# A conformer's last 256 channels, convolved as two halves of 128 tokens

## The chip, the cores and the metric

The kernel runs on one core of one Trainium2 chip. The metric is the device time of one execution in microseconds (us), and the figure quoted is the median over runs. In the rows below PE is TensorE's matrix multiplication, PEld its weight loads, DVE is VectorE, ACT is ScalarE, POOL is GpSimd, and SP is SyncE, which issues most DMA.

## The reference, cut to what matters

The program computes two blocks of a network over one sequence of 256 tokens with 1024 features, in float32. The first block has four layers; layer 1 mixes tokens with this conformer convolution (one of it in the program), and an MLP follows:

```python
def causal_depthwise_conv(x, w):
    k = w.shape[0]                       # 31 taps, one weight per tap and channel
    return lax.conv_general_dilated(x, w[:, None, :], window_strides=(1,),
        padding=[(k - 1, 0)], dimension_numbers=("NWC", "WIO", "NWC"),
        feature_group_count=x.shape[-1])

def conformer_conv_mixer(x, w_pw1, b_pw1, w_dw, b_dw, ln_g, ln_b, w_pw2, b_pw2):
    h = x @ w_pw1 + b_pw1
    a, gate = jnp.split(h, 2, axis=-1)
    h = a * jax.nn.sigmoid(gate)
    h = causal_depthwise_conv(h, w_dw) + b_dw
    mean = jnp.mean(h, axis=-1, keepdims=True)
    var = jnp.mean(jnp.square(h - mean), axis=-1, keepdims=True)
    h = (h - mean) * lax.rsqrt(var + LN_EPS) * ln_g + ln_b
    h = jax.nn.silu(h)
    return h @ w_pw2 + b_pw2
```

The LayerNorm is taken over all 1024 channels of a token, so it needs every channel's convolution, but only of that token.

## The kernel before

The 256 tokens are two halves, h = 0 and h = 1, of 128 tokens, one token per partition. Each half runs through a generator of its own. A driver hands both the same stream of weight units (128 x 1024 values, cast by ACT and DVE into a high part `wh`/`whx` and a low part `whl`/`whxl`); the second half lags five units behind the first in these layers. The multiplication is `mm3` (its matmuls are all on L59): three fp32r matmuls per 128 x 512 piece, `wh` and `whl` with the high part `t2h` of the activations, and `wh` with their low part `t2l`.

In the conformer (`conformer`), the first product gives 256 channels at a time, c = 0 to 3, with their gates, in a tile `cfr` per half. When both halves of a c are there, `depthwise` is put on a list of side work that is stepped between the products. For 256 channels and all 256 tokens it

- transposes the gates and the values (`tp<-ident,cfr`), takes the sigmoid on ACT (`cfs`) and multiplies on DVE into `win`, channels on partitions, 30 zeros ahead of the tokens;
- splits the 31 taps: for the first `CF_PE[c]` taps ACT (odd k) or POOL (even k) writes a diagonal matrix `dg` of that tap's weights, six buffers in turn, and PE multiplies it with the shifted window into PSUM (`mm<-win,dg`, plain float32); the other taps are multiply-adds on DVE into `cvo` (L711, started by L699), two blocks b of 128 channels each;
- adds the two sums (L715). For c = 3 the split is 15 taps on PE, 16 on DVE.

When the convolution of c = 3 is done, the half's generator goes on: the 1024 channels are transposed back (`tp<-ident,cvo`, L66), DVE takes the statistics (`bn`, L640), POOL the power (`rstd`, L411), DVE normalizes (`cfz`, L747), PE transposes again (`tp<-ident,cfz`), ACT applies SiLU (`cff`, L754) and casts (`t2h`, L351), DVE makes `t2l` (L352). This happens for two groups of 512 channels, and then the second product, eight weight units `cf2`, runs into `acc`. Half 1 does the same five units later.

Each engine executes its instructions in one fixed order; a scheduler settles that order when the program is built, from the order of the code and the buffers.

Of the kernel before, what the change touches and what calls it, by code (L numbers as in the profile page):

```python
# [10 lines left out]
F32 = mybir.dt.float32  # L11
# [4 lines left out]
ALU = mybir.AluOpType  # L16
# [3 lines left out]

PACE = {"1": (5, 2, 8), "A": (5, 2, 8), "M": (0, 4, 6), "B": (3, 2, 6), "P": (6, 1, 8)}

CF_PE = (10, 11, 13, 15)
RAWP, WHP = 3, 4
EXTRA = {"1": (2, 4), "A": (2, 4), "M": (0, 2)}

# [24 lines left out]
class Builder:  # L51
# [616 lines left out]
        s.segs.append((len(s.plan), None, None))  # L668
        s.plan_linear(s.io["cf_w_pw2"][j], 8, "cf2")

    def depthwise(s, c, raws):

        nc, sh = s.nc, s.sh
        on_pe = CF_PE[c]
        yield
        tg = s.tpb((128, 2, 2, 128))
        for h in range(2):
            for b in range(2):
                nc.tensor.transpose(tg[:, h, b, :], raws[h][:, 256 + 128 * b:384 + 128 * b], s.ident)
        sg = s.B2((128, 2, 2, 128), "cfs")  # L680
        for b in range(2):
            q = 2 * c + b
            nc.scalar.activation(sg[:, :, b, :], tg[:, :, b, :], AF.Sigmoid, bias=s.cfb1[:, 8 + q:9 + q])
        ta = s.tpb((128, 2, 2, 128))
        for h in range(2):
            for b in range(2):
                nc.tensor.transpose(ta[:, h, b, :], raws[h][:, 128 * b:128 * b + 128], s.ident)
        win = s.pool.tile([128, 2, 286], F32, tag="win", bufs=2, name="win")
        nc.gpsimd.memset(win[:, :, 0:30], 0.0)
        for b in range(2):  # L690
            q = 2 * c + b
            nc.vector.scalar_tensor_tensor(win[:, b, 30:286].rearrange("p (h t) -> p h t", h=2), ta[:, :, b, :],
                                           s.cfb1[:, q:q + 1], sg[:, :, b, :], op0=ALU.add, op1=ALU.mult)
        o = s.B2((128, 2, 256), "cvo")
        ps = s.mmb((128, 2, 256))
        for b in range(2):
            w = s.cfw[:, 2 * c + b, :]
            yield
            nc.vector.tensor_scalar(o[:, b, :], win[:, b, on_pe:on_pe + 256], w[:, on_pe:on_pe + 1],  # L699
                                    s.cfbd[:, 2 * c + b:2 * c + b + 1], op0=ALU.mult, op1=ALU.add)  # L700
            rest = list(range(on_pe + 1, 31))
            for k in range(on_pe):
                dg = s.pool.tile([128, 128], F32, tag="dg", bufs=6, name="dg")
                if k % 2:
                    nc.scalar.mul(dg, s.ident, w[:, k:k + 1])
                else:
                    nc.gpsimd.tensor_scalar(dg, s.ident, w[:, k:k + 1], None, op0=ALU.mult)
                nc.tensor.matmul(ps[:, b, :], dg, win[:, b, k:k + 256], start=k == 0, stop=k == on_pe - 1)
                n = len(rest) * (k + 1) // on_pe - len(rest) * k // on_pe
                for m in rest[len(rest) * k // on_pe:][:n]:  # L710
                    nc.vector.scalar_tensor_tensor(o[:, b, :], win[:, b, m:m + 256], w[:, m:m + 1], o[:, b, :],  # L711
                                                   op0=ALU.mult, op1=ALU.add)
                if k % 2:
                    yield
        nc.vector.tensor_tensor(o, o, ps, op=ALU.add)  # L715
        sh["cf", c] = o

    def conformer(s, h, lhs, rin, j):
        nc, sh = s.nc, s.sh
        for c in range(4):  # L720
            p = s.acc()
            for k in range(0, 8, 2):
                W = yield "cf1"
                for kk in range(2):
                    s.mm3(lhs, k + kk, W, [(p, kk * 512, 512, k + kk == 0, k + kk == 7)])
            t = s.B2(name="cfr")
            nc.scalar.mul(t, p, rin)
            sh["cfr", c, h] = t
            if h:
                s.side.append([s.depthwise(c, [sh.pop(("cfr", c, e)) for e in range(2)]), ("cf", c - 1) if c else None, 0.0])  # L730
        cb = s.layer_vec(("cb2", j), s.io["cf_b_pw2"][j])
        yield "#"
        while ("cf", 3) not in sh:
            s.side_step(False)
        t = slice(128 * h, 128 * h + 128)
        tps = []
        for g in range(2):
            p = s.tpb()
            for b in range(4):
                nc.tensor.transpose(p[:, b, :], sh["cf", 2 * g + b // 2][:, b % 2, t], s.ident)  # L740
            tps.append(p)
        flat = [p.rearrange("p b c -> p (b c)") for p in tps]
        r, m = s.ln_stats(flat, 1e-5)
        hT = []
        for c in range(2):
            z = s.B2(name="cfz")
            zi = nc.vector.tensor_scalar(z, flat[c], m, r, op0=ALU.subtract, op1=ALU.mult)  # L747
            if c == 0 and h == 0:
                s.hold = s.split_to, zi.ins
            tz = s.tr(z)  # L750
            f = s.B2((128, 4, 128), "cff")
            for b in range(4):
                q = 4 * c + b
                nc.scalar.activation(f[:, b, :], tz[:, b, :], AF.Silu, scale=s.cfg[:, q:q + 1], bias=s.cfbb[:, q:q + 1])  # L754
            hT.append(s.split(f))
        ps = yield from s.linear(hT, 8, "cf2")
        out = []
        for g in range(2):
            t = s.B2(name="cfo")
            nc.vector.tensor_tensor(t, ps[g], cb[g], op=ALU.add)  # L760
            out.append(t)
        return out
# [1148 lines left out]
```

## Time and profile before

| what | value |
|---|---|
| median of 3 runs | 2991.22 us (2991.18 to 2991.85) |
| the profiled execution's own time | 2988.3 us |
| its span, first to last instruction | 2986.5 us |
| PE busy | 2906.1 us, 97% of the span |
| DVE busy | 1982.2 us, 66% |
| ACT busy | 1522.5 us, 51% |
| POOL busy | 211.8 us, 7% |
| mean granted TensorE clock | 0.995 of full |

Busy time is an average over stages that differ: the change touches one stretch, from about 486 to 545 us after the span's start, and what counts there is which engine the others wait for. A granted clock of 1.00 is 2.4 GHz, 0.50 is 1.2 GHz. Matmuls of plain float32 stand in the trace as two records each.

### The profile page before, as it was taken

To read this page: it belongs to the slowest core of one execution; us is meant where nothing else is said; L and a number is where in the kernel's file an instruction comes from. 1 tells how busy PE (TensorE), PEld (TensorE's weight loads), DVE (VectorE), ACT (ScalarE), POOL (GpSimd) and SP (SyncE) were. 2 spreads that over 40 slices of the span, in tenths; PEclk is the share of its full clock that TensorE was granted. 3 is DMA by queue.
4 is the path that set the end of the run, shared out by engine and by line. 5 is a ranking of instruction groups with operands and counts; after the bars stand their busy time and mean duration, and the time that the engine had idled before them with its cause. 6 is when DMAs were issued, how large, how long until landed. Compare 5 with 4: busy or idle time off the path is not lost. (4 is left out here: it accounts for less than half of the span.)

```text
span 2986.5 us, 49201 instructions
## 1 busy us (share of the span) xinstructions
PE 2906.1 (97%) x18698; PEld 2335.4 (78%) x18698; DVE 1982.2 (66%) x3159; ACT 1522.5 (51%) x2348; POOL 211.8 (7%) x352
## 2 busy tenths in 40 slices
PE   8999998999999999999999999999999999999998
PEld 6778877787788878888877777878778787777886
DVE  7666678666766766766557757665665676667656
ACT  4354554555544534544447664444444387544443
POOL 0000024000000000200001000000010000000000
PEclk9999999999999999999999999999999999999999
DMA  7457852687578655886766233477667552334773
GB/s 240 155 175 236 240 164 78 191 238 213 177 233 241 188 169 169 239 250 198 224 196 184 75 114 108 127 220 224 212 207 224 160 173 87 100 113 140 238 225 125
DMA packets 342733, 542.64 MB, mean 182 GB/s; under 512 B 71381, under 2 KB 205729, under 8 KB 342496
## 3 DMA queue, kind: packets, MB, share of 16 engines
q1 hardware_dynamic: 333824, 514.90, 57.4%
q0 software_dynamic: 8096, 22.49, 2.6%
q8 instruction: 147, 2.41, 0.3%
q10 hardware_dynamic: 576, 2.10, 0.2%
q14 instruction: 90, 0.74, 0.1%
HBM read 516.30 MB, written 23.07 MB: 181 GB/s over the span
## 5 line engine op out<-in xcount | busy, mean ns | idle before, releaser
L59 PE MATMUL acc<-wh,t2h 128*128 128x512 f32 (+1 forms) x1512 | 610.8, 404 | 9.9 <-ACT t2h L351 7.3
L59 PE MATMUL acc<-whl,t2h 128*128 128x512 f32 (+1 forms) x1512 | 593.7, 393 | 0.4 <-DVE whl L224 0.4
L224 DVE TENSOR_TENSOR whl<-raw,wh 128x1024 fp32r<-128x1024 f32 x341 | 414.5, 1217 | 244.9 <-ACT wh L223 221.7
L223 ACT CAST wh<-raw 128x1024 fp32r<-128x1024 f32 x341 | 356.9, 1047 | 392.6 <-PE acc L59 246.5
L59 PE MATMUL acc<-wh,t2l 128*128 128x512 f32 (+1 forms) x1512 | 512.3, 395 | 3.1 <-DVE t2l L352 2.2
L224 DVE TENSOR_TENSOR whxl<-raw,whx 128x1024 fp32r<-128x1024 f32 x272 | 329.7, 1214 | 217.4 <-ACT whx L223 190.7
L223 ACT CAST whx<-raw 128x1024 fp32r<-128x1024 f32 x272 | 284.3, 1046 | 291.7 <-PE acc L59 135.4
L59 PEld LDWEIGHTS acc<-wh,t2h 128*128 128x128 f32 x1512 | 285.7, 189 | 82.5 <-ACT t2h L351 17.9
L59 PE MATMUL acc<-whx,t2h 128*128 128x512 f32 (+1 forms) x856 | 343.9, 403 | 2.1 <-ACT t2h L351 1.4
L59 PEld LDWEIGHTS acc<-wh,t2l 128*128 128x128 f32 x1512 | 283.6, 189 | 69.8 <-DVE t2l L352 9.2
L59 PE MATMUL acc<-whxl,t2h 128*128 128x512 f32 (+1 forms) x856 | 335.4, 392 | 0.1
L59 PEld LDWEIGHTS acc<-whl,t2h 128*128 128x128 f32 x1512 | 285.7, 189 | 55.7 <-issue 1.0
L59 PE MATMUL mm<-whx,t2h 128*128 128x512 f32 x800 | 313.4, 392 | 3.1 <-ACT whx L223 2.5
L59 PE MATMUL mm<-whxl,t2h 128*128 128x512 f32 x800 | 311.7, 390 | 0.8 <-DVE whxl L224 0.8
L59 PE MATMUL mm<-whx,t2l 128*128 128x512 f32 x800 | 311.6, 389 | 0.6 <-DVE t2l L352 0.6
L59 PE MATMUL acc<-whx,t2l 128*128 128x512 f32 (+1 forms) x856 | 282.4, 391 | 1.1 <-DVE var L644 0.7
L224 DVE TENSOR_TENSOR whxl<-rawx,whx 128x1024 fp32r<-128x1024 f32 x142 | 173.0, 1219 | 127.5 <-ACT whx L223 116.8
L224 DVE TENSOR_TENSOR whl<-rawx,wh 128x1024 fp32r<-128x1024 f32 x145 | 177.2, 1222 | 110.4 <-ACT wh L223 97.5
L223 ACT CAST whx<-rawx 128x1024 fp32r<-128x1024 f32 x142 | 148.8, 1050 | 158.9 <-PE mm L59 92.3
L223 ACT CAST wh<-rawx 128x1024 fp32r<-128x1024 f32 x145 | 152.2, 1051 | 151.2 <-PE acc L59 101.5
L59 PEld LDWEIGHTS acc<-whx,t2h 128*128 128x128 f32 x856 | 161.3, 188 | 39.7 <-ACT t2h L351 5.5
L59 PEld LDWEIGHTS acc<-whx,t2l 128*128 128x128 f32 x856 | 160.4, 188 | 38.0 <-DVE t2l L352 2.6
(617 smaller groups left out, 4103.3 us busy)
## 6 DMA issues: line engine op xcount, KB each, us to landing
raw<-in_mlp_w SPq DMA_DIRECT2D x153, 512.0 KB, 4.6
raw<-in_w_in SPq DMA_DIRECT2D x128, 512.0 KB, 3.7
raw<-in_ffn_w SPq DMA_DIRECT2D x216, 256.0 KB, 3.7
rawx<-in_mlp_w SPq DMA_DIRECT2D x103, 512.0 KB, 4.6
rawx<-in_ffn_w SPq DMA_DIRECT2D x136, 256.0 KB, 3.9
raw<-in_ret_w_in SPq DMA_DIRECT2D x58, 512.0 KB, 4.5
raw<-in_ffn_w SPq DMA_DIRECT2D x53, 512.0 KB, 4.2
rawx<-in_ret_w_in SPq DMA_DIRECT2D x38, 512.0 KB, 4.4
```

The costliest lines, as they stand in the source:

```text
L59: r = m0(out, a, b, **k)
L223: c = nc.scalar.copy(wh[:, 0:n], r[:, 0:n])
L224: nc.vector.tensor_tensor(wl[:, 0:n], r[:, 0:n], wh[:, 0:n].bitcast(F32), op=ALU.subtract)
```

## The change

For c = 3, `depthwise` is called once per half of the tokens instead of once for both. The first call makes `win` and the output tile `o`, computes tokens 0 to 127 and leaves both tiles for the second call, which computes tokens 128 to 255. Half 0's generator waits for ("cf", 3, 0) alone, and half 1's for ("cf", 3, 1). The second call may start once the first is done. The number of taps on PE for c = 3 goes from 15 to 17, and in the calls for one half ACT writes three of four `dg` tiles instead of one of two.

```diff
-CF_PE = (10, 11, 13, 15)
+CF_PE = (10, 11, 13, 17)
...
-    def depthwise(s, c, raws):
+    def depthwise(s, c, raws, halves=(0, 1)):
...
+        nh = len(halves)
         yield
-        tg = s.tpb((128, 2, 2, 128))
-        for h in range(2):
+        tg = s.tpb((128, nh, 2, 128))
+        for h in range(nh):
...
-        win = s.pool.tile([128, 2, 286], F32, tag="win", bufs=2, name="win")
-        nc.gpsimd.memset(win[:, :, 0:30], 0.0)
+        if halves[0] == 0:
+            win = s.pool.tile([128, 2, 286], F32, tag="win", bufs=2, name="win")
+            nc.gpsimd.memset(win[:, :, 0:30], 0.0)
+            o = s.B2((128, 2, 256), "cvo")
+            sh["cfw", c] = win, o
+        else:
+            win, o = sh.pop(("cfw", c))
+        t0, n = 128 * halves[0], 128 * nh
...
-        ps = s.mmb((128, 2, 256))
+        ps = s.mmb((128, 2, n))
         for b in range(2):
             w = s.cfw[:, 2 * c + b, :]
+            at = lambda k: win[:, b, k + t0:k + t0 + n]
+            ob = o[:, b, t0:t0 + n]
...
-                if k % 2:
+                if k % 2 or nh == 1 and k % 4:
                     nc.scalar.mul(dg, s.ident, w[:, k:k + 1])
                 else:
                     nc.gpsimd.tensor_scalar(dg, s.ident, w[:, k:k + 1], None, op0=ALU.mult)
-                nc.tensor.matmul(ps[:, b, :], dg, win[:, b, k:k + 256], start=k == 0, stop=k == on_pe - 1)
+                nc.tensor.matmul(ps[:, b, :], dg, at(k), start=k == 0, stop=k == on_pe - 1)
...
-        nc.vector.tensor_tensor(o, o, ps, op=ALU.add)
-        sh["cf", c] = o
+        nc.vector.tensor_tensor(o[:, :, t0:t0 + n], o[:, :, t0:t0 + n], ps, op=ALU.add)
+        for h in halves:
+            sh["cf", c, h] = o
...
-            if h:
-                s.side.append([s.depthwise(c, [sh.pop(("cfr", c, e)) for e in range(2)]), ("cf", c - 1) if c else None, 0.0])
+            if c == 3:
+                s.side.append([s.depthwise(c, [sh.pop(("cfr", c, h))], (h,)), ("cf", *((3, 0) if h else (2, 1))), 0.0])
+            elif h:
+                s.side.append([s.depthwise(c, [sh.pop(("cfr", c, e)) for e in range(2)]), ("cf", c - 1, 1) if c else None, 0.0])
...
-        while ("cf", 3) not in sh:
+        while ("cf", 3, h) not in sh:
             s.side_step(False)
```

What stands in the engines' queues moves in one place of the program. On PE, at the convolution of c = 3 (`dg`) and its neighbours, the difference reads:

```order
 L59 MATMUL mm<-win,dg 128x256 x22
-L66 MATMUL tp<-ident,cfr 128x128 x8
+L66 MATMUL tp<-ident,cfr 128x128 x4
 L66 MATMUL tp<-ident,cvo 128x128 x4
-L59 MATMUL mm<-win,dg 128x256 x30
+L59 MATMUL mm<-win,dg 128x128 x34
 L66 MATMUL tp<-ident,cvo 128x128 x4
 L66 MATMUL tp<-ident,cfz 128x128 x4
```

So 30 matmuls over 256 tokens became 34 over 128 ahead of half 0's LayerNorm, and the other half's transposes are gone from there.

Further down PE's queue, in half 0's second product (`acc<-wh`, units 3 to 5 of it), the changed kernel has:

```order
L59 MATMUL mm<-win,dg 128x128 x6
L59 MATMUL acc<-wh,t2l 128x512 x2
L59 MATMUL mm<-win,dg 128x128 x2
...
L59 MATMUL acc<-whx,t2l 128x512 x2
L59 MATMUL mm<-win,dg 128x128 x4
...
L59 MATMUL acc<-whx,t2l 128x512 x2
L59 MATMUL mm<-win,dg 128x128 x22
L66 MATMUL tp<-ident,cvo 128x128 x8
```

All 34 matmuls of the second half's convolution stand here, behind half 0's whole LayerNorm chain and its first three units, and ahead of half 1's `cvo` transposes. Four more `cfr` transposes stand just before, among units 1 and 2. In the kernel before, nothing but the products of units 0 to 5 stood ahead of `tp<-ident,cvo 128x128 x8`.

On ACT, from the first half's diagonals to half 1's SiLU, the changed kernel has:

```order
L714 ACTIVATE dg<-ident,cfc 128x128 x24
L765 ACT_TABLE_LOAD
L765 ACTIVATE cff<-tp,cfc 128x128 x4
L351 CAST t2h<-cff 128x512
L223 CAST whx<-raw 128x1024
L765 ACTIVATE cff<-tp,cfc 128x128 x4
L351 CAST t2h<-cff 128x512
L685 ACT_TABLE_LOAD
L685 ACTIVATE cfs<-tp,cfc 128x128 x2
L714 ACTIVATE dg<-ident,cfc 128x128 x20
L765 ACT_TABLE_LOAD
L765 ACTIVATE cff<-tp,cfc 128x128 x4
```

Before, the last `cff` x4 followed the second `t2h` directly; the sigmoid of the second half with two table loads and 20 diagonals now stand between. DVE's queue has the same form: `win` x2, L708 x2, L720 x26 and the sum of the second half stand behind half 0's second `t2l` and ahead of half 1's `bn`. Behind half 1's LayerNorm the rows of all engines are those of before.

## Rows read from the trace of the kernel before

**Rows 1.** Stretches: us; busy PE, PEld, DVE, ACT, POOL (count); clock, DMA share, GB/s.

```profile
487.00:500.00 13.00, 13.00 (x60) 11.38 (x61) 13.00 (x33) 5.70 (x12) 10.96 (x13) 1.00 0.01 2
500.00:508.00 8.00, 1.94 (x9) 1.06 (x7) 6.71 (x11) 1.59 (x5) 0.57 (x1) 0.76 0.08 13
508.00:515.00 7.00, 6.05 (x17) 4.50 (x18) 5.87 (x7) 3.71 (x7) 0.00 (x0) 0.54 0.93 320
515.00:520.00 5.00, 5.00 (x24) 4.12 (x23) 0.06 (x1) 0.00 (x0) 0.00 (x0) 1.00 0.46 160
...
527.00:533.00 6.00, 5.74 (x20) 4.67 (x21) 2.64 (x3) 3.39 (x7) 0.00 (x0) 0.72 0.04 5
```

**Rows 2.** What PE waited for from 470 to 570: total us, times, longest.

```profile
PE acc L59 <- ACT t2h L351: 4.3, 2, 2.2
PE tp L66 <- DVE cfz L747: 3.6, 3, 2.8
```

**Rows 3.** Timeline of DVE: start, duration, instruction, idle before and its releaser.

```profile
486.39 0.47 DVE L692 SCALAR_TENSOR_TENSOR win<-tp,cfc,cfs 128x256 f32<-128x256 f32 x1
...
487.77 0.72 DVE L699 TENSOR_SCALAR cvo<-win,cfc 128x256 f32<-128x256 f32 x2
488.42 12.34 DVE L711 SCALAR_TENSOR_TENSOR cvo<-win,cfc,cvo 128x256 f32<-128x256 f32 x30
500.68 0.69 DVE L640 BATCH_NORM_STATS2 bn<-tp 128x6 f32<-128x512 f32 x1
501.28 0.66 DVE L715 TENSOR_TENSOR cvo<-cvo,mm 128x512 f32<-128x512 f32 x1
```

**Rows 4.** Timeline of PE over the same stretch.

```profile
487.00 13.19 PE L59 MATMUL mm<-win,dg 128*128 128x256 f32 x60 [0.69 <-DVE win L692]
...
508.59 0.79 PE L59 MATMUL acc<-wh,t2h 128*128 128x512 f32 x1 [2.25 <-ACT t2h L351]
```

**Rows 5.** DVE groups by form: count, busy us, mean ns, idle before.

```profile
L1478 DVE SCALAR_TENSOR_TENSOR gcv<-win,rwpar,gcv 128x128 f32<-128x128 f32 x144 | 38.9, 344 | 2.2 <-ACT gcv L1476 2.1
L901 DVE TENSOR_TENSOR glu<-silu,mm 128x256 f32<-128x256 f32 x88 | 35.8, 407 | 4.6 <-ACT silu L899 4.6
...
L802 DVE SCALAR_TENSOR_TENSOR scu<-swin,cfc,scu 128x128 f32<-128x128 f32 x32 | 9.1, 343 | 0.0
...
L800 DVE TENSOR_SCALAR scu<-swin,cfc 128x128 f32<-128x128 f32 x16 | 3.8, 280 | 0.5 <-ACT swin L796 0.4
```

**Rows 6.** Timeline of PE at 102 us, float32 matmuls of 128 columns.

```profile
101.94 1.95 PE L59 MATMUL mm<-rT 128*128 128x128 f32 x16
103.64 0.48 PE L59 MATMUL acc<-wh,t2h 128*128 128x512 f32 x1
```

**Rows 7.** Timeline of ACT at 457 us: two diagonals in a row.

```profile
457.42 0.75 ACT L705 ACTIVATE dg<-ident,cfc 128x128 f32<-128x128 f32 x2
```

**Rows 8.** Timeline of POOL during the convolution of c = 3.

```profile
487.77 10.96 POOL L707 TENSOR_SCALAR dg<-ident,cfc 128x128 f32<-128x128 f32 x13 [2.14 <-PE mm L59]
```

**Rows 9.** Timeline of PE at half 1's transposes.

```profile
520.40 1.03 PE L66 MATMUL tp<-ident,cvo 128*128 128x128 f32 x8
```

**Rows 10.** Timeline of ACT between the convolution and half 1.

```profile
497.63 1.28 ACT L754 ACT_TABLE_LOAD   x1
...
513.72 0.62 ACT L351 CAST t2h<-cff 128x512 fp32r<-128x512 f32 x1
```

**Rows 11.** The sigmoid on ACT, grouped by form.

```profile
L683 ACT ACTIVATE cfs<-tp,cfc 128x256 f32<-128x256 f32 x8 | 3.4, 472 | 0.0
```

**Rows 12.** Timeline of DVE at half 1's statistics.

```profile
521.03 1.29 DVE L640 BATCH_NORM_STATS2 bn<-tp 128x6 f32<-128x512 f32 x2 [5.98 <-PE tp L66]
```

**Rows 13.** Weight loads of the matmuls of rows 6, grouped over the span.

```profile
L59 PEld LDWEIGHTS mm<-rT 128*128 128x128 f32 x96 | 11.3, 192 | 0.3
```

**Rows 14.** Two more stretches, columns as in the first group.

```profile
1960.00:1962.00 2.00, 0.57 (x2) 0.49 (x3) 2.00 (x4) 1.67 (x2) 0.00 (x0) 1.00 0.22 73
2366.00:2372.00 6.00, 5.14 (x16) 3.83 (x17) 3.91 (x12) 3.28 (x5) 0.00 (x0) 0.72 0.56 125
```

More of the change, by code (lines that the diff above doesn't have):

```diff
@@ L669, in plan_cf @@
         s.plan_linear(s.io["cf_w_pw2"][j], 8, "cf2")
-    def depthwise(s, c, raws):
+    def depthwise(s, c, raws, halves=(0, 1)):
         nc, sh = s.nc, s.sh
         on_pe = CF_PE[c]
+        nh = len(halves)
         yield
-        tg = s.tpb((128, 2, 2, 128))
-        for h in range(2):
+        tg = s.tpb((128, nh, 2, 128))
+        for h in range(nh):
             for b in range(2):
                 nc.tensor.transpose(tg[:, h, b, :], raws[h][:, 256 + 128 * b:384 + 128 * b], s.ident)
-        sg = s.B2((128, 2, 2, 128), "cfs")
+        sg = s.B2((128, 2, 2, 128), "cfs")[:, 0:nh]
         for b in range(2):
@@ L683, in depthwise @@
             nc.scalar.activation(sg[:, :, b, :], tg[:, :, b, :], AF.Sigmoid, bias=s.cfb1[:, 8 + q:9 + q])
-        ta = s.tpb((128, 2, 2, 128))
-        for h in range(2):
+        ta = s.tpb((128, nh, 2, 128))
+        for h in range(nh):
             for b in range(2):
                 nc.tensor.transpose(ta[:, h, b, :], raws[h][:, 128 * b:128 * b + 128], s.ident)
-        win = s.pool.tile([128, 2, 286], F32, tag="win", bufs=2, name="win")
-        nc.gpsimd.memset(win[:, :, 0:30], 0.0)
+        if halves[0] == 0:
[6 more added lines that the diff above has]
+        t0, n = 128 * halves[0], 128 * nh
         for b in range(2):
             q = 2 * c + b
-            nc.vector.scalar_tensor_tensor(win[:, b, 30:286].rearrange("p (h t) -> p h t", h=2), ta[:, :, b, :],
+            nc.vector.scalar_tensor_tensor(win[:, b, 30 + t0:30 + t0 + n].rearrange("p (h t) -> p h t", h=nh), ta[:, :, b, :],
                                            s.cfb1[:, q:q + 1], sg[:, :, b, :], op0=ALU.add, op1=ALU.mult)
-        o = s.B2((128, 2, 256), "cvo")
-        ps = s.mmb((128, 2, 256))
+        ps = s.mmb((128, 2, n))
         for b in range(2):
             w = s.cfw[:, 2 * c + b, :]
+            at = lambda k: win[:, b, k + t0:k + t0 + n]
+            ob = o[:, b, t0:t0 + n]
             yield
-            nc.vector.tensor_scalar(o[:, b, :], win[:, b, on_pe:on_pe + 256], w[:, on_pe:on_pe + 1],
+            nc.vector.tensor_scalar(ob, at(on_pe), w[:, on_pe:on_pe + 1],
                                     s.cfbd[:, 2 * c + b:2 * c + b + 1], op0=ALU.mult, op1=ALU.add)
@@ L707, in depthwise @@
                     nc.gpsimd.tensor_scalar(dg, s.ident, w[:, k:k + 1], None, op0=ALU.mult)
-                nc.tensor.matmul(ps[:, b, :], dg, win[:, b, k:k + 256], start=k == 0, stop=k == on_pe - 1)
[L709 to L712, printed above, removed]
+                nc.tensor.matmul(ps[:, b, :], dg, at(k), start=k == 0, stop=k == on_pe - 1)
+                m0, m1 = (len(rest) * x // on_pe for x in (k, k + 1))
+                for m in rest[m0:m1]:
+                    nc.vector.scalar_tensor_tensor(ob, at(m), w[:, m:m + 1], ob, op0=ALU.mult, op1=ALU.add)
                 if k % 2:
                     yield
-        nc.vector.tensor_tensor(o, o, ps, op=ALU.add)
-        sh["cf", c] = o
+        nc.vector.tensor_tensor(o[:, :, t0:t0 + n], o[:, :, t0:t0 + n], ps, op=ALU.add)
+        for h in halves:
+            sh["cf", c, h] = o
     def conformer(s, h, lhs, rin, j):
@@ L739, in conformer @@
             for b in range(4):
-                nc.tensor.transpose(p[:, b, :], sh["cf", 2 * g + b // 2][:, b % 2, t], s.ident)
+                nc.tensor.transpose(p[:, b, :], sh["cf", 2 * g + b // 2, h][:, b % 2, t], s.ident)
             tps.append(p)
```

## The prediction

> **What bounds the kernel now.** I read the table of stretches around the conformer first [rows 1]. From 487 to 500 us DVE is busy for all 13.00 us and PE too: the multiply-adds of c = 3 and its diagonal matmuls run side by side. From 500 to 508 PE works 1.94 of 8 us: half 0's LayerNorm chain. From 508 to 515 it is busy again, at a granted clock of 0.54, so mostly at 1.2 GHz. From 515 to 520 it has no gap, at 2.4 GHz. Then the list of PE's waits [rows 2]: `t2h` 4.3 us in two waits, `cfz` 3.6 in three. So the stretch is a chain: DVE's convolution, then the LayerNorm from engine to engine with PE idle, then PE alone. What a change does here is read from when two things happen: the end of the sum that half 0 waits for, and the `bn` of half 1.
>
> The timeline of DVE gives the first date [rows 3]: `win` at 486.39, the multiply-adds from 488.42 on for 12.34 us, half 0's first `bn` at 500.68, the sum at 501.28, done at 501.94. PE's matmuls of that convolution start at 487.00 and end at 500.19 [rows 4], so DVE is the later one. PE's first product of half 0 starts at 508.59 [rows 4], 6.65 us after the sum.
>
> **What the change removes: half a convolution ahead of half 0.** DVE's part starts where it did, at 486.39, since the convolution of c = 2 ahead of it is untouched. Then, with the durations of 128-column instructions elsewhere [rows 5]: two `win` at 9.1/32 = 0.28 us each, 0.57; the sum of c = 2 as before, 0.66 at most [rows 3]; two starts at 3.8/16 = 0.24, 0.48; 26 multiply-adds (13 taps, two blocks) at 0.284, 7.39. That is 495.5. Then `bn`, 0.60 from its start to the next instruction's, and the sum over 256 elements, 0.41 (35.8/88). It ends at 496.5 instead of 501.94: **-5.4 us**. Halving the columns does not halve DVE's time: 256 columns took 12.34/30 = 0.41 per tap, 128 take 0.28.
>
> The other three engines must not be later. PE: 34 matmuls of two records each. Sixteen such records took 1.95 us, and the next matmul started 1.70 after the first of them [rows 6]: between 0.106 and 0.122 per record. I take 0.112, so 0.224 per matmul, 7.6 us in all, done by 494.6 from a start at 487.0. ACT: 20 of its 24 diagonals come after the start (four are written ahead into the six buffers); two in a row took 0.75, so 0.35 from one to the next [rows 7], 7.0 us, at most 0.40, 8.0: 494.3 to 495.3. POOL: eight diagonals at 10.96/13 = 0.84 [rows 8], 6.7 us. All end before DVE's 495.5, ACT by little. The bounds: 0.27 per multiply-add, as in another tap loop (38.9/144 [rows 5]), gives -5.8; a small sum at the old 0.66 with PE held up by ACT to 496 gives -5.0.
>
> From there to half 0's first product the queues read as before, with the same instructions (the first six diagonals for the second half now stand on ACT and POOL ahead of SiLU and power, but they need only the buffers that the convolution's last matmuls free, so they are done about when the sum is). So `t2h`, PE's restart, the idle stretch and the low clock in it come 5.4 us earlier, and cost the same.
>
> **What it adds: the second half of the convolution, in PE's queue between half 0's units.** The order of PE's queue decides this. The 34 matmuls don't stand in the idle stretch of the LayerNorm, but behind it, in 515 to 520, where PE has no gap [rows 1], and ahead of the `cvo` transposes at 520.40 [rows 9] that half 1 starts from. So they are paid in full: 34 x 0.224 = 7.6 us. The four `cfr` transposes beside them: eight transposes took 1.03 us [rows 9], so 0.5 for four, and 0.65 if two are at the low clock. Do they wait? The window needs ACT: the second `t2h` ends at 514.34, a table load takes 1.28 [rows 10], two sigmoids at most 0.47 each [rows 11], two `win` 0.57, so 517.1 on the clock of before. PE gets to its first diagonal behind unit 3's four high matmuls, 14 matmuls ahead of 520.40, some 3 us at the rate of 515 to 520 (24 in 5.00 us [rows 1]), and 0.65 later for the transposes: 518. No wait. The last 22 matmuls stand together; six diagonals are ready, and ACT has to write 12 of the other 16 at 0.35 to 0.40. Counted through buffer by buffer this ends 0.25 us later than PE alone would, 0.8 at 0.40. DVE's multiply-adds (7.39 + 0.48 from 517.1) end at 525, over 3 us before PE. The last sum, 0.41, lies beside the first six transposes (0.65). So half 1's `bn`, at 521.03 [rows 12], comes **+8.5 us** later on the clock of before (8.0 with 0.106 per record, 9.3 with 0.122). ACT's second table load, 1.28 us, stands behind the last diagonal; the SiLU that needs it comes after transposes, two `bn` (1.29 alone [rows 12]), power and `cfz`, so it is hidden.
>
> Behind half 1's `bn` every queue is that of before, and each step there waits for this chain or for the casts that follow it; the weight loads behind it are issued when the casts free buffers, and move along. So the rest moves as one piece.
>
> **Sum.** -5.4 + 8.5 = +3.1 us, bounds +2.2 to +4.3. The profiled execution took 2988.3 us, its span 2986.5; the median is 2.9 above it, which I add unchanged: 2991.2 + 3.1 = **2994.3 us**, 0.1% more. A measurement of this kernel can tell about 0.2%, 6 us, from no change, so this is "the same".
>
> **A rule against it.** The Trainium skill, "TensorE: Matmul & The Clock Gate", section "Back-to-back issue gap", says that a stream of weight loads and matmuls is paced by both, 81 ns per pair at 128 columns, more than the columns alone would take. If each record here is two such pairs, an estimate from that figure is 0.32 us per matmul instead of 0.224, and the sum would be some +8 us. The 0.112 per record in rows 6 was with a new weight load for each, so the trace does not agree for that reading.
>
> **Rivals.**
> *Weight loads set the pace* (slower). Each matmul over 128 columns loads as many weights as one over 256. A load lasts 0.192 [rows 13]; if loads don't hide behind the shorter matmuls, a matmul takes 0.384 and half a convolution 13.1 on PE. The first half then ends at 500.1, the sum at 500.5 (-1.4), the second adds 0.16 x 34 = 5.4 to 8.5: +12.5, 3003.7 us. It passes +6 us from about 0.29 per matmul on (above 0.27 PE also outlasts DVE in the first half). For it: PE was never asked for this beside DVE, ACT and POOL together. Against: rows 6, same shape, loads overlapped.
>
> *The clock falls elsewhere.* In 527 to 533 the mean granted clock was 0.72, so 1.2 GHz for 0.28 x 2 x 6 = 3.4 us, which costs 1.7. The same happened at 2366 [rows 14], but not at 1960, where PE worked 0.57 of 2 us [rows 14]. From 500 to 515 it was low for 3.8 + 6.4 = 10.3 us. Such stretches come and go with where the gaps fall, and the change moves all of them by 3 us. One or two more: +4.8 or +6.5, 2996 to 2998. One or two fewer: +1.4 or -0.3, 2991 to 2993. Nothing in the profile says which; the gaps themselves stay as long as they were.
>
> *The convolution is hidden* (the change does what its name says). If the second half's matmuls ran in PE's two long waits for half 0's LayerNorm, 2.8 and 2.2 us [rows 2], 5.0 of the 8.5 would go: +3.1 - 5.0 = -1.9, 2989.3 us, still within 0.2%. The PE order speaks against it: the matmuls keep the place that the queue gives them.
>
> **How the numbers follow.** The forecast as summed, 0.5; one or two clock stretches fewer, 0.13; more, 0.2 (a quarter of it beyond 6 us); weight loads 0.08; hidden 0.04; something that I don't see 0.05, half to each side. Slower: 0.05 + 0.08 + 0.025 = 0.15. Faster: 0.03. Same: 0.82. The range runs from the hidden convolution, 2989.3, which is also just below the low bound with two low stretches fewer (2990.0), to the high bound with two more, 2998.9. It leaves out the weight-load rival and the tail. The forecast's own range is that of the sum, 2993.4 to 2995.5.
>
> **What would show it.** In the changed kernel's trace: half 0's sum ends near 496.5 and its first product starts near 503.2; the diagonal matmuls have 0.112 us per record in the first half; 68 more records of `mm<-win,dg` lie between half 0's `acc` rows; half 1's `bn` starts near 524 instead of 521.03; PE's waits for `t2h` and `cfz` are as long as in rows 2. I am wrong if the records take 0.15 or more, if `win` of the second half makes PE wait, if half 1's LayerNorm is delayed by something other than PE's queue, or if the low clock takes much more or less than in rows 1.

## The result, and the profile after

The changed kernel took 3007.56 us (median of 5 runs, 3004.7 to 3009.3) where the kernel before, run beside it, took 2991.18 (2988.39 to 2991.85). The ratio is 1.0057, with a 95% interval of 1.0044 to 1.007. So the change costs 16.4 us. The forecast, 2994.3 with a range of 2989.3 to 2998.9, is wrong: the time lies 8.7 us above the range. The profiled execution took 3008.57 us, with a span of 3006.8.

The list of PE's waits around the conformer (470 to 580 us; total us, times, longest) is read first. It answers to [rows 2].

```profile
PE mm L59 <- POOL dg L716: 9.3, 2, 6.5
PE acc L59 <- ACT t2h L351: 4.3, 2, 2.2
PE tp L66 <- DVE cfz L758: 3.6, 3, 2.8
```

`t2h` and `cfz` are as before. The first line is new: TensorE waited twice, 9.3 us together, for a diagonal that POOL had to write. In the kernel before there is no such line.

The timeline of POOL at these two places, and its diagonals from 487 us on as one group (shortest/median/longest in ns):

```profile
487.52 7.44 POOL L716 TENSOR_SCALAR dg<-ident,cfc 128x128 f32<-128x128 f32 x1 [3.11 <-PE mm L59]
520.95 5.48 POOL L716 TENSOR_SCALAR dg<-ident,cfc 128x128 f32<-128x128 f32 x1 [14.73 <-PE mm L59]
L716 POOL TENSOR_SCALAR dg<-ident,cfc x18: 594/602/7437, 487.5 to 534.3; 128x128 f32<-128x128 f32 x18
```

One diagonal, 0.60 us of work in the median, took 7.44 us in the first half and one took 5.48 in the second. Such a diagonal is called caught below, and the moment at which POOL begins on a diagonal its request. Before, 13 of them took 10.96 us [rows 8]. DVE's timeline says what ran meanwhile (it answers to [rows 3] and [rows 12]):

```profile
487.59 6.91 DVE L720 SCALAR_TENSOR_TENSOR cvo<-win,cfc,cvo 128x128 f32<-128x128 f32 x26
494.41 0.69 DVE L640 BATCH_NORM_STATS2 bn<-tp 128x6 f32<-128x512 f32 x1
503.48 0.42 DVE L723 TENSOR_TENSOR cvo<-cvo,mm 128x256 f32<-128x256 f32 x1 [8.38 <-PE mm L59]
...
519.04 6.91 DVE L720 SCALAR_TENSOR_TENSOR cvo<-win,cfc,cvo 128x128 f32<-128x128 f32 x26
535.56 0.42 DVE L723 TENSOR_TENSOR cvo<-cvo,mm 128x256 f32<-128x256 f32 x1 [9.61 <-PE mm L59]
535.99 1.29 DVE L640 BATCH_NORM_STATS2 bn<-tp 128x6 f32<-128x512 f32 x2
```

The long diagonal of the first half begins at 487.52, just ahead of DVE's 26 multiply-adds, and ends at 494.96, 0.46 us after the last of them (487.59 + 6.91 = 494.50). In the second half it ends at 526.43, and the stream at 525.95. DVE wasn't held at all: 6.91/26 = 0.266 us each, and 6.90 for the 26 in run 1 below, where POOL had nothing to do beside them. It then stood idle for 8.38 and 9.61 us, waiting for TensorE's sum.

TensorE's timeline (it answers to [rows 4]) shows what that does to the dates:

```profile
486.45 2.02 PE L59 MATMUL mm<-win,dg 128*128 128x128 f32 x16 [0.92 <-DVE win L700]
495.01 8.43 PE L59 MATMUL mm<-win,dg 128*128 128x128 f32 x52 [6.54 <-POOL dg L716]
510.54 0.79 PE L59 MATMUL acc<-wh,t2h 128*128 128x512 f32 x1 [2.24 <-ACT t2h L351]
...
542.24 0.50 PE L59 MATMUL acc<-wh,t2h 128*128 128x512 f32 x1 [2.02 <-ACT t2h L351]
```

After 16 records it stops for 6.54 us. The first half's sum ends at 503.90 (503.48 + 0.42) instead of 501.94, half 0's first product starts at 510.54 instead of 508.59, and half 1's at 542.24 instead of 527.26 (the last in the timeline of before): 15.0 us later. Of the table of stretches one row answers to [rows 1]:

```profile
486.00:500.00 14.00, 7.01 (x39) 6.85 (x40) 9.10 (x33) 4.69 (x13) 9.80 (x5) 0.76 0.01 2
```

TensorE worked 7.01 of 14 us here, at a mean granted clock of 0.76, so at 1.2 GHz for 0.24 x 2 x 14 = 6.7 us, where before it had no gap from 487 on and full clock. So part of the first half's delay is the lower clock behind the stop: the 52 records then took 8.43/52 = 0.162 us each, the 16 ahead of it 2.02/16 = 0.126. POOL reads as busy for 9.80 us, with 5 instructions. A busy share alone would have looked like an engine that has much to do.

### The profile page after: what moved, and what is told of

It is laid out like the page before. It is cut to its first block, busy times and chain, and to the rows that moved or that the text cites. A ratio compares the mean times of both kernels' runs of the same rounds, so it can differ in the third digit from the quotient of the medians.

```text
span 3006.8 us, 49424 instructions
## 1 busy us (share of the span) xinstructions
PE 2918.4 (97%) x18774; PEld 2347.2 (78%) x18774; DVE 1985.3 (66%) x3186; ACT 1535.8 (51%) x2386; POOL 222.7 (7%) x356
```

## The experiments

Twelve runs in all. Each ratio is to the kernel before, run on the same chip beside it.

| kernel | median us | before | ratio, 95% interval |
|---|---|---|---|
| changed | 3007.56 | 2991.18 | 1.0057 (1.0044 to 1.007) |
| 1 changed, half calls' diagonals on ACT alone | 2994.57 | 2991.47 | 1.0007 (0.9998 to 1.0017) |
| 2 before, multiply-adds of c = 3 split in two | 2995.70 | 2991.47 | 1.0012 (1.0003 to 1.0021) |
| 3 changed, DVE's sums in PSUM | 2996.01 | 2991.47 | 1.0014 (1.0005 to 1.0024) |
| 4 before, 17 taps on TensorE | 2993.57 | 2991.47 | 1.0003 (0.9994 to 1.0013) |
| 5 changed, blocks alternate | 3001.62 | 2990.34 | 1.0048 (1.0031 to 1.0065) |
| 6 before, split in two, as a chain | 2994.53 | 2990.34 | 1.0017 (1.0008 to 1.0027) |
| 7 second half between LayerNorm's steps | 2995.18 | 2990.34 | 1.0015 (1.0006 to 1.0025) |
| 8 as 5, one sum in PSUM | 2997.08 | 2992.00 | 1.0016 (1.0006 to 1.0025) |
| 9 changed, POOL's taps shifted | 3000.10 | 2992.00 | 1.0029 (1.0018 to 1.0039) |
| 10 as 7, first half's diagonals on ACT | 2986.59 | 2992.00 | 0.9984 (0.9975 to 0.9993) |
| 11 as 5, once more | 3004.82 | 2987.51 | one execution each |
| 12 changed, once more | 3008.72 | 2987.51 | one execution each |

The first theory was that POOL's diagonals are shut out while DVE streams short multiply-adds. Its rivals were TensorE's own work in the halves (weight loads, clock) and the 17 taps.

### 1. No diagonals on POOL

```diff
-                if k % 2 or nh == 1 and k % 4:
+                if k % 2 or nh == 1:
```

> The changed kernel with all 34 diagonals of each half call made on ScalarE, none on GpSimd. Theory (GpSimd's diagonals are shut out while VectorE streams its 26 multiply-adds over 128 columns): TensorE's 9.3 us of waits for dg from GpSimd go, ScalarE sets the pace at about 0.36 each (rows 7 of the profile before: 0.75 for two), 34 x 0.36 = 12.2 us from 486.9, so the first half's sum stands near 499.5 instead of 503.9, the second half's statistics at 527 to 531 instead of 536.0, and the whole near 2999 (2995 to 3003). Rival (TensorE's own work in the halves, its weight loads or its clock, makes the loss, and the wait for GpSimd only covers it): sum and statistics within 1.5 us of 503.9 and 536.0, the whole near 3007.

Timelines of ACT, DVE and PE in this run:

```profile
487.09 10.04 ACT L714 ACTIVATE dg<-ident,cfc 128x128 f32<-128x128 f32 x34 [2.02 <-PE mm L59]
495.95 0.42 DVE L723 TENSOR_TENSOR cvo<-cvo,mm 128x256 f32<-128x256 f32 x1 [0.71 <-PE mm L59]
503.01 0.79 PE L59 MATMUL acc<-wh,t2h 128*128 128x512 f32 x1 [2.25 <-ACT t2h L351]
530.57 0.50 PE L59 MATMUL acc<-wh,t2h 128*128 128x512 f32 x1 [2.25 <-ACT t2h L351]
```

The wait is gone, though ACT has more to do. The sum ends at 496.37, 7.5 us ahead of the changed kernel's, half 1's first product starts 11.7 us ahead, and the median is 13.0 us lower. That refutes the rivals: TensorE has the same 136 records to do. The gain was expected too small: the sum came 3.1 us earlier than expected and the whole some 4 us lower. A diagonal cost ACT 10.04/34 = 0.295 us, not 0.36, and of the 34 in this row only 28 are the first half's (six of its 34 were written ahead, and the last six here are already the second half's).

### 2 and 6. Short multiply-adds in the kernel before

Run 2 does each 256-column multiply-add of c = 3 as two of 128 columns:

```diff
-                    nc.vector.scalar_tensor_tensor(o[:, b, :], win[:, b, m:m + 256], w[:, m:m + 1], o[:, b, :],
-                                                   op0=ALU.mult, op1=ALU.add)
+                    for e in ((0, 128), (128, 256)) if c == 3 else ((0, 256),):
+                        nc.vector.scalar_tensor_tensor(o[:, b, e[0]:e[1]], win[:, b, m + e[0]:m + e[1]], w[:, m:m + 1], o[:, b, e[0]:e[1]],
+                                                       op0=ALU.mult, op1=ALU.add)
```

> The kernel before, with one edit: each multiply-add of the last group's convolution on VectorE is two instructions of 128 columns instead of one of 256; diagonals, TensorE's products and all order stay. Theory (short back-to-back two-input instructions shut GpSimd out): 60 instructions x 0.27 = 16.2 us of stream from 486.4, in it GpSimd ends at most two or three of its 16 diagonals and makes the others after it at 0.60 each, so the sum stands at 507 to 512 instead of 501.9, TensorE waits for dg from GpSimd by over 5 us, and the whole is 5 to 10 us slower. Rival (only VectorE's own longer time counts): the sum at 503 to 505 (60 x 0.27 against 30 x 0.41, 3.9 us more on VectorE alone), GpSimd keeps 0.84 a diagonal, and the whole is 1 to 3.5 us slower.

DVE's stream, and POOL's diagonals from 487 us on as one group:

```profile
489.76 16.70 DVE L712 SCALAR_TENSOR_TENSOR cvo<-win,cfc,cvo 128x128 f32<-128x128 f32 x60
...
507.00 0.67 DVE L716 TENSOR_TENSOR cvo<-cvo,mm 128x512 f32<-128x512 f32 x1
```

```profile
L707 POOL TENSOR_SCALAR dg<-ident,cfc x13: 655/724/941, 489.1 to 499.1; 128x128 f32<-128x128 f32 x13
```

The theory fails in this form. Beside 60 of the same short instructions POOL wrote 13 diagonals, none longer than 0.94 us. The loss is of the kind that the rival said, DVE's own longer stream, but larger: the sum was done at 507.67 where the rival had 503 to 505, and the median is 4.2 us up where it had 1 to 3.5. In this execution the stream also began 1.3 us later than in the profile of before. One difference from the changed kernel is that here a multiply-add doesn't read its neighbour's result. Run 6 takes that away, by doing all 15 taps over the first 128 columns and then all over the others:

```diff
...
+            if c == 3:
+                rest = [(m, e, e + 128) for e in (0, 128) for m in range(on_pe + 1, 31)]
...
```

> The kernel before with each multiply-add of the last group as two of 128 columns, as in the run that split it, but in the order of a chain: of a block first all 15 taps over columns 0 to 127, then all 15 over columns 128 to 255, so that each reads its neighbour's result. Theory D: GpSimd is shut out for most of the 60 instructions (16 us) but where the chain changes its columns, which is four times: at most 5 diagonals in the stream, TensorE waits over 5 us for them, the sum at 510 or later, the whole 8 us or more slower than before. Rival (a phase of the two engines that this place does not have): GpSimd keeps 0.7 to 0.9, the sum near 507.7 as in the split run, the whole 3 to 6 us slower than before.

```profile
L709 POOL TENSOR_SCALAR dg<-ident,cfc x14: 658/746/939, 486.2 to 499.1; 128x128 f32<-128x128 f32 x14
```

The same again: a chain by itself doesn't shut POOL out either. Another difference is left in both runs. POOL's first diagonal began at 489.12 and 489.14, ahead of the multiply-adds (489.76 and 489.79), and each further one within 0.2 us of the last, while in the changed kernel the caught ones followed 3.11 and 14.73 us of idle time.

### 3. DVE's sum in PSUM

```diff
+        oc = s.mmb((128, 2, n)) if nh == 1 else None
...
-            ob = o[:, b, t0:t0 + n]
+            ob = o[:, b, t0:t0 + n] if nh == 2 else oc[:, b, :]
...
+        if nh == 1:
+            nc.scalar.copy(o[:, :, t0:t0 + n], oc)
```

> The changed kernel, with VectorE's accumulator of the half calls in PSUM instead of SBUF (a second bank; ScalarE copies it out before the last add), so that a multiply-add reads one tensor from SBUF and one from PSUM. Theory, form A (GpSimd is shut out by instructions with two SBUF tensors): GpSimd's diagonals come at 0.6 to 0.85 through the stream, TensorE's waits for dg fall below 2 us, the first half's sum stands at 496 to 499, the second half's statistics at 523 to 527, the whole near 2995 (2990 to 2999). Form B (any gap-free stream of short VectorE instructions shuts GpSimd out, wherever the accumulator lies): GpSimd waits through the stream as now, sum at 503 to 505, the whole 3006 to 3010. Rival (weight loads or clock): as form B in the time, but with GpSimd's diagonals running at 0.6 to 0.85 in the stream.

DVE's first block, and POOL's diagonals as one group:

```profile
488.47 5.03 DVE L721 SCALAR_TENSOR_TENSOR mm<-win,cfc,mm 128x128 f32<-128x128 f32 x13
```

```profile
L717 POOL TENSOR_SCALAR dg<-ident,cfc x18: 602/603/612, 488.9 to 525.1; 128x128 f32<-128x128 f32 x18
```

Form A holds for POOL: all 18 diagonals take 0.60 to 0.61 us, as if DVE were not there. So what holds POOL goes with two tensors of a multiply-add in SBUF; but this stream is slower too, and run 8 below takes that difference away. The Trainium skill, "SBUF — State Buffer", section "Who interferes with whom", says this: a DVE instruction with two SBUF inputs contends with a GpSimd instruction that reads SBUF, and one with at most one, outside DVE's two-port performance modes, does not. The runs agree, with 0.603 us beside PSUM sums, and 7.44 beside SBUF sums in the same place. The price is on DVE, 5.03/13 = 0.387 us per multiply-add instead of 0.266. So the sum ended at 499.90, 0.9 us later than expected, and the second half's last statistics began at 528.64 instead of by 527.

### 4. The 17 taps alone

```diff
-CF_PE = (10, 11, 13, 15)
+CF_PE = (10, 11, 13, 17)
```

> One part of the change alone: the kernel before with 17 instead of 15 taps of the last group on TensorE, 256 columns at once, diagonals shared out as before. Theory: the moved taps cost little, since GpSimd gets a diagonal through every 0.84 us beside multiply-adds over 256 columns: 18 of them on GpSimd instead of 16 make the sum about 1.7 us later, four multiply-adds fewer on VectorE 1.6 us earlier there; the sum within 2 us of 501.9, the whole within 3 us of before. Rival (17 taps on TensorE, not the halving, make the loss): the sum 5 us or more later, the whole over 5 us slower.

```profile
488.32 10.76 DVE L711 SCALAR_TENSOR_TENSOR cvo<-win,cfc,cvo 128x256 f32<-128x256 f32 x26
501.88 0.69 DVE L715 TENSOR_TENSOR cvo<-cvo,mm 128x512 f32<-128x512 f32 x1 [2.19 <-PE mm L59]
```

The sum ends at 502.57 instead of 501.94, and the time is the same within what can be measured. So the taps don't make the loss.

### 5 and 11. The same instructions in another order, twice

The multiply-adds of a half call alternate between the two blocks of 128 channels, so that neighbours are independent (the start of both sums stands ahead of them):

```diff
...
+            if nh == 1:
+                rest = [(m, e) for m in range(on_pe + 1, 31) for e in (0, 1)][len(rest) * b:][:len(rest)]
...
```

> The changed kernel with the same 26 multiply-adds of each half call in another order: they alternate between the two blocks of 128 channels, so that no multiply-add reads what its neighbour has just written; everything else as changed. Theory D (GpSimd is shut out by a chain of 128-column multiply-adds each of which reads its neighbour's result): GpSimd's diagonals come in 0.65 to 0.95 within the stream, TensorE's waits for dg from GpSimd go below 1.5 us, the first half's sum stands at 494.5 to 497, the second half's last statistics at 523 to 526, the whole near 2994 (2990 to 2998). Rival (the place decides, for instance that VectorE's stream and GpSimd start together, not the chain): a diagonal of about 7 us again, sum at 503 to 505, the whole 3005 to 3010.

POOL's timeline, in the first half and at the start of the second, and TensorE's at half 1's first product:

```profile
487.93 7.44 POOL L718 TENSOR_SCALAR dg<-ident,cfc 128x128 f32<-128x128 f32 x1 [3.11 <-PE mm L59]
...
520.61 0.83 POOL L718 TENSOR_SCALAR dg<-ident,cfc 128x128 f32<-128x128 f32 x1 [13.53 <-PE mm L59]
521.89 0.89 POOL L718 TENSOR_SCALAR dg<-ident,cfc 128x128 f32<-128x128 f32 x1 [0.45 <-PE mm L59]
...
537.37 0.50 PE L59 MATMUL acc<-wh,t2h 128*128 128x512 f32 x1 [2.02 <-ACT t2h L351]
```

Theory D, that the chain decides, falls: the first half is caught as before, the second is not, with the same order in both. The four times of this kernel lie 12.7 us apart (2995.87 to 3008.57). So a third theory, L: a request can miss every boundary of the stream or none, and the moment at which it comes decides. Then the same program need not do the same twice.

> The alternating order once more, unchanged, for one more profiled execution. Its four times so far lie 12.7 us apart (2995.87 to 3008.57), and the profiled one, the fastest, had one half caught. Theory L (the moment of a request decides, and it is not the same in every execution): the number of caught halves may differ from the first profile, and the time goes with it, 2992 to 2999 with one half or none, 3000 to 3010 with two. Rival (the spread of the times has another cause): again the first half caught and the second free, whatever the time.

```profile
489.56 8.02 POOL L718 TENSOR_SCALAR dg<-ident,cfc 128x128 f32<-128x128 f32 x2 [3.11 <-PE mm L59]
...
521.66 6.52 POOL L718 TENSOR_SCALAR dg<-ident,cfc 128x128 f32<-128x128 f32 x2 [14.29 <-PE mm L59]
...
543.36 0.50 PE L59 MATMUL acc<-wh,t2h 128*128 128x512 f32 x1 [2.02 <-ACT t2h L351]
```

Unchanged instructions, and now both halves are caught (in each row two diagonals share the time, one of them long), at 3004.82 us instead of 2995.87. Half 1's first product starts 6.0 us later than in run 5. Order and form are the same in both executions, so neither decides, and the rival falls. Theory L fits; that it is the moment which decides isn't shown by this. The two executions also ran on different chips; the four times of run 5 are of one chip, but only one of them was profiled.

### 8 and 9. A way in, and another moment

Run 8 puts the second block's sum alone into PSUM, on top of run 5, so that every other multiply-add reads one SBUF tensor:

```diff
+        oc = s.mmb((128, n)) if nh == 1 else None
+        part = lambda e: oc if nh == 1 and e else o[:, e, t0:t0 + n]
...
```

> The run with the alternating order, with the accumulator of the second block of 128 channels in PSUM (ScalarE copies it out at the end): every other multiply-add of the stream then reads one tensor from SBUF, the ones between still two. Theory L (a diagonal of GpSimd can miss the boundaries between multiply-adds with two SBUF tensors again and again, and only an instruction without two of them lets it in for certain): every diagonal of both halves takes 0.6 to 1.2, none over 1.5; TensorE waits for dg from GpSimd under 1.5 us in sum; the first half's sum at 496 to 499, the second half's last statistics at 524 to 528, the whole 2993 to 2998, within 3 us of the run with both accumulators in PSUM. Rival (any stream without a gap shuts GpSimd out once it is caught): a diagonal of 7 us in the first half again, the whole above 3000.

```profile
L720 POOL TENSOR_SCALAR dg<-ident,cfc x18: 598/603/867, 488.9 to 522.4; 128x128 f32<-128x128 f32 x18
```

No diagonal is longer than 0.87 us, and DVE doesn't pay for it as in run 3 (the last line is TensorE's):

```profile
487.96 0.33 DVE L725 SCALAR_TENSOR_TENSOR cvo<-win,cfc,cvo 128x128 f32<-128x128 f32 x1
488.22 0.34 DVE L725 SCALAR_TENSOR_TENSOR mm<-win,cfc,mm 128x128 f32<-128x128 f32 x1
...
530.38 0.50 PE L59 MATMUL acc<-wh,t2h 128*128 128x512 f32 x1 [2.01 <-ACT t2h L351]
```

The starts are 0.26 us apart, as in the changed kernel, and POOL gets in all the same. So it wasn't the slower pace that let it in in run 3. Run 9 leaves DVE as changed, and only moves POOL's requests (taps 2, 6, 10, 14 instead of 0, 4, 8, 12, 16):

```diff
-                if k % 2 or nh == 1 and k % 4:
+                if k % 2 or nh == 1 and k % 4 != 2:
```

> The changed kernel, where GpSimd makes the diagonals of taps 2, 6, 10 and 14 of a block instead of 0, 4, 8, 12 and 16 (8 instead of 10 in a half), ScalarE the others: GpSimd's first request in each stream comes at another moment against VectorE's instructions, and VectorE's instructions and their order stay. Theory L, where the moment of the request decides: one half or both may go free; a request is either granted within 1.1 us or not until the stream ends, nothing between, and with none caught the whole is near 2995, with both near 3006. Rival S (a stream of these instructions shuts GpSimd out always): both halves are caught whatever the moment, first half's sum at 502 or later and second half's statistics at 532 or later, the whole 3003 to 3009.

```profile
486.98 0.60 POOL L716 TENSOR_SCALAR dg<-ident,cfc 128x128 f32<-128x128 f32 x1 [3.79 <-PE mm L59]
487.88 1.54 POOL L716 TENSOR_SCALAR dg<-ident,cfc 128x128 f32<-128x128 f32 x2 [0.29 <-ACT dg L714]
...
512.52 5.83 POOL L716 TENSOR_SCALAR dg<-ident,cfc 128x128 f32<-128x128 f32 x1 [14.37 <-PE mm L59]
```

```profile
487.61 7.30 DVE L720 SCALAR_TENSOR_TENSOR cvo<-win,cfc,cvo 128x128 f32<-128x128 f32 x26
...
495.44 0.40 DVE L723 TENSOR_TENSOR cvo<-cvo,mm 128x256 f32<-128x256 f32 x1
...
529.78 0.42 DVE L723 TENSOR_TENSOR cvo<-cvo,mm 128x256 f32<-128x256 f32 x1 [11.91 <-PE mm L59]
```

The first half is now free, and its sum is done at 495.84: POOL's first diagonal ended ahead of the stream, and those within it got in, for which DVE paid with 7.30 us instead of 6.91. The second half is caught for 5.83 us, to the end of the stream, and half 1's first product starts at 536.47. That refutes rival S: the same stream, in the same place, catches POOL or doesn't. The time lies between, at 1.0029.

### 12. The changed kernel once more

> The changed kernel once more, for a second profile. Its five times lie 4.6 us apart (3004.7 to 3009.3), all about 13 us above the run with the diagonals on ScalarE alone. Theory L with a moment that this program repeats: both halves caught again, a diagonal of 7 us in the first and of 5 to 7 us in the second, the whole 3004 to 3010; with one half free instead, 2996 to 3002. Rival (the caught halves of the first profile are an accident of that execution and not what the five times are made of): at most one half caught, and the time at 3004 or more all the same.

```profile
489.39 8.02 POOL L716 TENSOR_SCALAR dg<-ident,cfc 128x128 f32<-128x128 f32 x2 [3.11 <-PE mm L59]
...
521.74 6.42 POOL L716 TENSOR_SCALAR dg<-ident,cfc 128x128 f32<-128x128 f32 x2 [14.37 <-PE mm L59]
```

Both halves are caught again, and TensorE waits 9.6 us for `dg`. In the first half POOL had stood idle for the same 3.11 us ahead of the request in runs 5, 11 and 12 and in the first profile; it began 0.06 to 0.07 us ahead of the first multiply-add, and was caught each time. In the second half that idle time differs from one to the next (14.73, 13.53, 14.29 and 14.37 us), and with 13.53 POOL went free. That the moment repeats in the one and not in the other fits theory L, but is read from these few executions only.

Half 1's first product goes with the number of caught halves. Against 527.26 before it comes 3.1 and 3.3 us later where none is caught at the same pace of DVE (runs 8 and 1), 9.2 and 10.1 with one (runs 9 and 5), and 15.0 to 16.1 with two (the first profile, and runs 11 and 12).

### 7 and 10. A version that beats both

The second half's convolution is written between the steps of the first half's LayerNorm, with run 5's order, so that its matmuls stand where TensorE waits:

```diff
+        ss = lambda n: [s.side_step(False) for _ in range(n)] if h == 0 else None
+        ss(2)
         t = slice(128 * h, 128 * h + 128)
...
         r, m = s.ln_stats(flat, 1e-5)
+        ss(3)
...
+            ss(3)
             tz = s.tr(z)
...
             hT.append(s.split(f))
+            ss(3)
```

> A try at a version that beats both: the alternating order, and the second half's convolution is written between the steps of the first half's LayerNorm instead of between its products, so that TensorE's 34 matmuls of the second half fall into the 12 us in which it waits for the first half's LayerNorm (waits of 2.8, 2.2 and more in the profile before) instead of standing in its queue among the products. Expected: first half's first product at 503 to 506, second half's first product at 522 to 526 instead of 527.3 before, the whole 1 to 6 us under before (2985 to 2990). Rival (VectorE's and ScalarE's work of the second half delays the first half's LayerNorm by as much): the first product at 508 or later, the whole within 2 us of before.

```profile
487.99 7.01 POOL L718 TENSOR_SCALAR dg<-ident,cfc 128x128 f32<-128x128 f32 x1 [3.54 <-ACT dg L716]
```

The first half was caught for 7.01 us. Its sum was done at 504.68, its first product started at 514.02, and the gain was lost: 1.0015. So ACT got the first half's diagonals:

```diff
-                if k % 2 or nh == 1 and k % 4:
+                if k % 2 or halves == (0,) or nh == 1 and k % 4:
```

> The version with the second half's convolution written between the steps of the first half's LayerNorm, now with all 34 diagonals of the first half on ScalarE, since there GpSimd was caught for 7.0 us in that run (first half's sum at 504.3, first product at 514.0). Expected: first half's sum at 496 to 497 as in the run with ScalarE alone, first product at 505.5 to 507.5, second half's first product 8 us earlier than in that run, the whole at 2985 to 2989 where before has 2991. Rival (ScalarE, with the second half's diagonals ahead of the first half's SiLU, or VectorE's multiply-adds ahead of the second cfz, sets the pace): first product at 508.6 or later, the whole 2990 or more.

```profile
496.00 0.42 DVE L726 TENSOR_TENSOR cvo<-cvo,mm 128x256 f32<-128x256 f32 x1
...
496.47 0.61 PE L59 MATMUL mm<-win,dg 128*128 128x128 f32 x4
...
497.36 3.72 PE L59 MATMUL mm<-win,dg 128*128 128x128 f32 x30
...
501.39 1.50 PE L59 MATMUL mm<-win,dg 128*128 128x128 f32 x12
504.68 0.49 PE L59 MATMUL mm<-win,dg 128*128 128x128 f32 x2 [1.78 <-ACT dg L716]
505.18 0.50 PE L59 MATMUL acc<-wh,t2h 128*128 128x512 f32 x1
...
524.70 0.50 PE L59 MATMUL acc<-wh,t2h 128*128 128x512 f32 x1 [2.02 <-ACT t2h L351]
```

48 of the second half's 68 records lie between the first half's sum and its first product, which starts at 505.18, 3.4 us earlier than before. From the sum to this product it is 8.8 us instead of 6.65, so the rival holds in part: the second half's work delays the first half's LayerNorm, by less than was won. Half 1's product starts at 524.70, 2.6 us earlier. The ratio is 0.9984 (0.9975 to 0.9993), 5.4 us by the medians. The interval, 2.1 to 7.5 us, holds the 2.6 too. In the profiled executions the lead is still 2.0 us at 2360 us and 5.3 at 2386: there TensorE's clock fell in the execution of before [rows 14], and in run 10's it didn't (1.00 from 2355 to 2395). So halving paid here where the second half stood in the LayerNorm's gaps and ScalarE wrote the first half's diagonals. Some of the second half's were still POOL's, beside a stream with gaps, and took at most 1.39 us.

## Why the prediction was wrong

**The step that failed** is the one on POOL: "eight diagonals at 10.96/13 = 0.84 [rows 8], 6.7 us. All end before DVE's 495.5". The 0.84 came from diagonals beside multiply-adds over 256 columns, and I carried it over to a stream of shorter ones. It is right when the request gets in (0.60 to 0.94 in runs 2, 6 and the free half of 9). The changed kernel's first request in each half didn't, one diagonal took 7.44 us and one 5.48, and TensorE waited 9.3 us for them, a wait that the prediction put at nothing. The rivals didn't have this case at all, though the rule quoted in run 3 names exactly these two instructions.

**The other terms, by run 1**, in which POOL is out of the way. The sum was forecast at 496.5 and ended at 496.37; half 0's first product at 503.2, measured 503.01. Half 1's first product was to come 3.1 us later than before, and came 3.3 later. The median was forecast at 2994.3, and run 1 has 2994.57. So halving the convolution did cost what the sum says, and the caught diagonals cost the rest: 7.5 us in the first half (503.90 against 496.37), and 4.1 more up to half 1's first product (11.7 in all). That the first date fits to 0.1 us is partly luck: DVE was ready at 495.25, earlier than forecast, and the sum then waited 0.71 for TensorE, which ended at 495.92 instead of 494.6 because ACT had all the diagonals to write.

**The size of the pieces.** 26 multiply-adds took 6.91 us (7.39 forecast). TensorE's records took 0.13 us in run 1 (32 in 4.16) where I had 0.112; ACT was the pace there. Where the diagonals were ready they took 0.115 (44 in 5.07, second half of runs 3, 8, 9, 11 and 12). The 0.162 behind the stop in the changed kernel is above the 0.15 that I had named as a sign of being wrong, but at 1.2 GHz: the granted clock from 495 to 500 us was 0.50. So the rival on weight loads, which came nearest in time with 3003.7, was wrong in its mechanism: it needs 0.192 per record, and the 0.32 per matmul that I set against my sum wasn't seen either. `t2h` and `cfz` waited as forecast, 4.3 and 3.6 us.

**The rest of the loss.** 15.0 us are there by half 1's first product, and 16.4 lie between the medians, with an interval of 13.2 to 20.9 that holds both. The spans of the two profiled executions differ by 20.3. Of this the trace shows where it arises: the same cast of weights (`whl`) at 2400.74 us before and 2415.94 after is still 15.2 us apart, and the `t2l` at 2690.42 and 2710.77 is 20.4. Between them the changed kernel's execution had two stretches at 1.2 GHz, and that of before none (first row before, the others after):

```profile
2400.00:2700.00 300.00, 296.72 (x4180) 233.11 (x4179) 205.62 (x523) 195.95 (x417) 19.66 (x42) 1.00 0.38 111
2608.00:2620.00 12.00, 11.90 (x207) 8.34 (x206) 8.39 (x27) 5.75 (x23) 0.00 (x0) 0.86 0.32 89
2676.00:2690.00 14.00, 14.00 (x105) 10.84 (x104) 5.29 (x11) 5.82 (x19) 0.05 (x1) 0.88 0.32 105
```

That is 0.14 x 2 x 12 + 0.12 x 2 x 14 = 6.7 us at half clock, at most 3.4 us of delay; the other 1.8 stay open. So the rival on the clock was there too, but small beside the 15.0.

**What stays open of the mechanism.** That a request is caught or not, and that it then stays caught until the stream ends, is shown by nine catches in six executions. That two SBUF tensors are needed rests on runs 3 and 8, where all four streams let POOL in after 4 to 15 us of idle time, and where none of the nineteen times is above 2999.75. What decides for a stream with two SBUF tensors isn't shown. Caught requests within a stream began 0.07, 0.10, 0.14, 0.24 and 0.24 us after the start of a multiply-add (the first profile and runs 7, 11, 9 and 12), free ones 0.18 (run 5) and 0.01 to 0.21 (run 9, first half), so this offset alone doesn't separate them. How long POOL stood idle is a rival that no run separates from the moment: ten times a diagonal after at least 3 us of idle time met such a stream (one more, in run 10, met only its last multiply-add), and nine were caught; in the free halves of runs 5 and 9 none that followed the last within 1.4 us was.

## What to carry to other kernels

A duration read beside one partner holds for that partner: before carrying GpSimd's time over to another stream of VectorE, look whether both read SBUF and whether the stream has a gap. If TensorE needs what GpSimd writes, don't put it beside a gap-free stream of two-input VectorE instructions; let ScalarE write it, or give the stream an instruction with an operand in PSUM. And halving work to overlap it paid here only with the second half's instructions in the queue where the engine really waits.

## What the hardware showed that I had not expected

- A GpSimd instruction of 0.60 us that reads SBUF was held for 7.44, 7.01, 5.83 and 5.48 us beside streams of 128-column multiply-adds 0.266 us apart, to 0.5 us after the last one. The Trainium skill ("SBUF — State Buffer", section "Summary: rules for kernel authors") says that the one that comes second blocks until the other is through; here some twenty to twenty-six of them finished first. Beside the same instructions, where it got in, it took 0.60 to 1.01 (runs 5 and 9), and DVE's 26 then took 7.12 and 7.30 us instead of 6.91.
- The same program had one half caught in one execution (2995.87 us) and both in another (3004.82, on another chip).
- A chain of multiply-adds whose sum lies in PSUM ran at 0.387 us each, in SBUF at 0.266. In run 8, where a sum in SBUF and one in PSUM alternate, the starts were 0.26 apart.
